# A fused low-rank linear layer on one core: part of the first load goes to GpSimd's DMA queue, and the matmul loop takes in its last round

## The chip, the cores and the metric

The kernel runs on one core of a Trainium2 chip. The core has a matrix engine (TensorE, PE in the profile), a vector engine (VectorE, DVE), a scalar engine (ScalarE, ACT), GpSimd (POOL) and SyncE (SP), which only issues transfers here. Sixteen DMA engines carry all transfers between the device memory and the core's own memory (SBUF, 128 partitions), whichever engine issues them. The metric is the device time of one execution in microseconds (us); less is better. The profile shows one execution, and its span runs from the first to the last instruction that the profiler recorded.

## The reference: what is computed

```
x_flat = x.reshape(-1, in_dim)            # 32768 x 256, float32
y = x_flat @ W                            # W: 256 x 256
lora_out = x_flat @ lora_A                # lora_A: 256 x 16
lora_out = lora_out * lora_E              # lora_E: 16 numbers
lora_out = lora_out @ lora_B              # lora_B: 16 x 256
y = y + scale * lora_out                  # scale is 1.0; y is written as float32
```

x and the result are 33.55 MB each. Everything else is small: W is 256 KB, lora_A and lora_B 16 KB each, lora_E 64 bytes.

## The kernel before: how the work is laid out

The low-rank branch is folded into the weights once, before the main work. TensorE transposes lora_A (L125), VectorE scales the transposed rows by lora_E and by scale (`ate`, L129), TensorE multiplies that by lora_B (L134), and VectorE adds W to it (`weff`, L138). After that the kernel is one matrix product of x with `weff`, in bf16.

The 32768 rows of x are cut into nine chunks, listed in `PLAN` as rows per partition: 32 rows per partition are 4 MB, 16 are 2 MB. A partition's rows of a chunk lie next to each other in device memory, so one partition's share of a chunk is one piece of 32 KB or 16 KB. Six buffers of SBUF (`slots`) hold the chunks, and the result overwrites the chunk in place, so a buffer is free for the seventh, eighth and ninth chunk only when the store of its first user has landed.

SyncE's DMA queue carries W, all nine loads and all nine stores, in the order in which SyncE issues them. The first six loads (`LEAD`, L106) are issued before the engines' common starting barrier; lora_A, lora_B and lora_E are issued by ScalarE (L102 to L105). Behind the barrier SyncE issues the store of a chunk when ScalarE has written its last group (L209, L210). The entry `AFTER = {2: [6, 7, 8]}` puts the last three loads behind the third store: each of them waits until the store that frees its buffer has landed (L212, L213). The order on the queue is thus: six loads, three stores, three loads, six stores.

A chunk is worked on in groups of four rows per partition, 64 groups in all. VectorE rounds two groups at a time to bf16 (`rounded`, L148). TensorE transposes a group (`transposed`, L162), VectorE copies the transposed group out of the accumulator memory (`copied`, L154), TensorE multiplies it by `weff` (`multiplied`, L173), and ScalarE copies the product back over the chunk (L201). TensorE's program is a loop of 15 rounds of four groups (L189), and the sixteenth round is written out behind the loop (L193 to L196). The counters `can_t`, `can_m` and `can_y` let TensorE wait on constants inside the loop.

A transfer adds sixteen to its semaphore when it is done, one for each DMA engine, and the trace has the time of each of these sixteen steps.

Of the kernel before, what the change touches and what calls it, by code (L numbers as in the profile page):

```python
# [3 lines left out]

PLAN = [32] * 5 + [16, 16, 32, 32]
ROWS, SLOTS = 32, 6
LEAD = 6
AFTER = {2: [6, 7, 8]}

G, ROUND = 4, 4  # L10

B_PARTS = [(0, 16)]
P = 128
FP32 = mybir.dt.float32
BF16 = mybir.dt.bfloat16
# [15 lines left out]
def kernel(tc, x, W, lora_A, lora_B, lora_E, scale, out):  # L31
    nc = tc.nc
    x_flat = x.flatten_outer_dims()
# [4 lines left out]
    KC = K // P  # L38
    assert K == M and sum(PLAN) * P == N
    starts = [sum(PLAN[:i]) * P for i in range(len(PLAN))]  # L40

    groups = [(i, r) for i, b in enumerate(PLAN) for r in range(0, b, G)]
    NG = len(groups)
    assert NG % ROUND == 0

    def rows_of(flat, i):
        b, r0 = PLAN[i], starts[i]
        return flat[r0:r0 + b * P, :].rearrange("(p b) k -> p b k", b=b)

    def sbuf(name, shape, dt):  # L50
        return nc.alloc_sbuf_tensor(name, shape, dt).ap()

    def psum(name, shape, dt):
# [4 lines left out]
    e_sb = sbuf("e_sb", [R, 1], FP32)  # L58
# [9 lines left out]
    b_sb = xb[1][:R, G:G + 2, :].rearrange("p g k -> p (g k)").bitcast(FP32)  # L68
# [4 lines left out]
    ps_aeb = psum("ps_aeb", [P, KC, M], FP32)  # L73

    s_w, s_a, s_b, s_e = (Count(nc, f"s_{k}") for k in "wabe")
    s_ld = [Count(nc, f"s_ld{i}") for i in range(len(PLAN))]
    s_st = [Count(nc, f"s_st{i}") for i in range(len(PLAN))]
    s_id, s_set, s_v, s_t, s_m, s_y = (
        Count(nc, k) for k in ("s_id", "s_set", "s_v", "s_t", "s_m", "s_y"))


    can_t, can_m, can_y = (nc.alloc_semaphore(k) for k in ("can_t", "can_m", "can_y"))

    def slot(i):
        return slots[i % SLOTS][:, :PLAN[i], :]

    def load(i):
        s_ld[i].by(nc.sync.dma_start(out=slot(i), in_=rows_of(x_flat, i)), 16)
# [4 lines left out]
    def spent(engine, count):  # L93
        engine.wait_ge(count.sem, count.total).then_inc(count.sem, -count.total)

    def take(sem):
        nc.tensor.wait_ge(sem, 1).then_inc(sem, -1)  # L97


    with tc.tile_critical(no_gpsimd_drain=True):  # L100
        s_w.by(nc.sync.dma_start(out=w_sb, in_=W.rearrange("(c p) m -> p c m", p=P)), 16)
        s_a.by(nc.scalar.dma_start(out=a_sb, in_=lora_A.rearrange("(c p) r -> p c r", p=P)), 16)  # L102
        for lo, hi in B_PARTS:
            s_b.by(nc.scalar.dma_start(out=b_sb[lo:hi, :], in_=lora_B[lo:hi, :]), 16)
        s_e.by(nc.scalar.dma_start(out=e_sb, in_=lora_E[:, None]), 16)  # L105
        for i in range(LEAD):  # L106
            load(i)
    tc.close()
    tc.compile()  # L109
# [4 lines left out]
        out=ident, in_=ident, compare_op=mybir.AluOpType.not_equal, fill=1.0, base=0,  # L114
# [3 lines left out]


    nc.vector.wait_ge(s_b.sem, s_b.total)  # L120
    s_v.by(nc.vector.tensor_copy(out=b_bf, in_=b_sb))  # L121
    nc.tensor.wait_ge(s_a.sem, 16)
    nc.tensor.wait_ge(s_id.sem, 3)
    for c in range(KC):
# [5 lines left out]
        out=ate, in0=ps_at, scalar1=e_sb, scalar2=float(scale),  # L130
# [11 lines left out]
    def rounded(t):  # L142
        i, r = groups[2 * t]
        if r == 0:
            nc.vector.wait_ge(s_ld[i].sem, 16)
        if t >= 2:
            nc.vector.wait_ge(s_t.sem, 2 * t - 2)
        nc.vector.tensor_copy(out=xb[t % 2], in_=slot(i)[:, r:r + 2 * G, :]).then_inc(can_t, 1)  # L148

    def copied(g):  # L150
        nc.vector.wait_ge(s_t.sem, g + 1)
        if g >= 2:
            nc.vector.wait_ge(s_m.sem, g - 1)
        nc.vector.tensor_copy(out=xt[g % 2], in_=ps_xt[g % 2]).then_inc(can_m, 1)  # L154


    def transposed(k):
        if k % 2 == 0:
            take(can_t)
        for j in range(G):  # L160
            for c in range(KC):
                done = nc.tensor.transpose(  # L162
                    ps_xt[k % 2][:, j, c, :],
                    xb[k // 2 % 2][:, k % 2 * G + j, c * P:(c + 1) * P],
                    ident_bf)
        done.then_inc(s_t.sem, 1)

    def multiplied(k):
        take(can_m)
        take(can_y)  # L170
        for j in range(G):
            for c in range(KC):
                done = nc.tensor.matmul(  # L173
                    ps_y[k % 2][:, j, :], xt[k % 2][:, j, c, :], weff[:, c, :],
                    start=(c == 0), stop=(c == KC - 1))
        done.then_inc(s_m.sem, 1)

    rounded(0)
    nc.vector.wait_ge(s_v.sem, 3)
    rounded(1)  # L180
    nc.scalar.sem_inc(can_y, 2)
    for t in range(NG // 2):
        copied(2 * t)
        copied(2 * t + 1)
        if t + 2 < NG // 2:
            rounded(t + 2)

    transposed(0)
    with nc.tensor.Fori(0, NG // ROUND - 1):  # L189
        for k in range(ROUND):  # L190
            transposed((k + 1) % ROUND)
            multiplied(k)
    for k in range(ROUND):  # L193
        if k + 1 < ROUND:
            transposed(k + 1)
        multiplied(k)  # L196
    s_t.total = s_m.total = NG

    for g, (i, r) in enumerate(groups):
        nc.scalar.wait_ge(s_m.sem, g + 1)  # L200
# [21 lines left out]
    nc.tensor.wait_ge(can_y, 1).then_inc(can_y, -1)  # L222
    for count in [s_y] + s_st:
        spent(nc.sync, count)


# [33 lines left out]
```

## Time and profile before

| what | before |
|---|---|
| median of 3 runs (lowest, highest) | 164.19 us (164.1, 164.44) |
| the profiled execution, its own time | 164.33 us |
| its span | 162.9 us |
| busy share of TensorE / VectorE / ScalarE / GpSimd | 57% / 49% / 41% / 1% |
| moved by DMA, mean rate over the span | 67.45 MB, 414 GB/s |
| first 4 MB load, issue to landing (issued at 1.4 us) | 12.6 us |
| ScalarE's last copy ends | 130.9 us |
| last store, issue to landing (issued at 130.9 us) | 32.0 us |

The profiled execution took 1.43 us more than its span. The page draws the span as forty equal slices of 4.07 us; a digit is the busy share of an engine in that slice in tenths. The row "DMA" is the mean over the sixteen DMA engines, and "GB/s" is what they moved. The table of stretches gives the same for any stretch of the span; there a packet of a transfer is counted whole in the stretch in which it starts. A packet is here the piece of one partition: 32 KB or 16 KB for x.

### The profile page before, as it was taken

The page shows a single profiled execution, that of the slowest core. Times are in us where ns is not written, and L with a number is a line of the kernel's source. Part 1 is how long each engine was busy: PE and PEld are TensorE (multiplying, and loading weights), DVE is VectorE, ACT ScalarE, POOL GpSimd, SP SyncE. Part 2 cuts the span into 40 slices and gives each one's busy share as a digit, 9 for nine tenths or more (in the row PEclk, how much of TensorE's full clock was granted, in tenths as well). Part 3 has the DMA queues.
Part 4 walks back from the last instruction along what each step waited for, and adds up shares of the span by engine and source line. Part 5 has one row for each costly group of instructions (what it writes and reads, how often), then busy time and mean ns, then how long its engine had stood idle before and what let it go on. Part 6 is the DMA issues. An engine that isn't in the chain of part 4 may idle for free. (4 is left out here: it accounts for less than half of the span.)

```text
span 162.9 us, 2599 instructions
## 1 busy us (share of the span) xinstructions
PE 92.5 (57%) x1028; PEld 81.5 (50%) x1028; DVE 79.5 (49%) x99; ACT 66.1 (41%) x65; POOL 1.0 (1%) x7
## 2 busy tenths in 40 slices
PE   0112999999999999997000049599999800000000
PEld 0002789888988898896000038498889600000000
DVE  0025878898889888882000083588987300000000
ACT  0300277777777777777000004467777710000000
POOL 0100000000000000000000000000000000000000
PEclk9999999999999999999855556999999965555555
DMA  6999899999998999999999999999999999999991
GB/s 197 390 491 410 386 507 394 394 499 394 426 469 382 326 451 418 467 402 442 442 394 426 467 402 467 420 426 459 410 442 426 410 404 438 451 442 426 442 451 64
DMA packets 3205, 67.45 MB, mean 414 GB/s; under 512 B 625, under 2 KB 897, under 8 KB 897
## 3 DMA queue, kind: packets, MB, share of 16 engines
q1 hardware_dynamic: 2864, 67.37, 97.1%
q10 hardware_dynamic: 336, 0.03, 0.2%
q8 instruction: 1, 0.02, 0.0%
q14 instruction: 4, 0.02, 0.0%
HBM read 33.85 MB, written 33.55 MB: 414 GB/s over the span
## 5 line engine op out<-in xcount | busy, mean ns | idle before, releaser
L201 ACT COPY xy<-psum_y 128x1024 f32<-128x1024 f32 x64 | 64.8, 1012 | 59.3 <-PE psum_y L173 59.3
L173 PE MATMUL psum_y<-weff,xt 128*128 128x256 bf16 x512 | 68.7, 279 | 23.1 <-PEq L97 21.6
L173 PEld LDWEIGHTS psum_y<-weff,xt 128*128 128x128 bf16 x512 | 47.5, 99 | 31.2 <-issue 25.7
L154 DVE COPY xt<-psum_xt 128x1024 bf16<-128x1024 bf16 x64 | 43.8, 687 | 15.3 <-PE psum_xt L162 15.1
L148 DVE CAST xb<-xy 128x2048 bf16<-128x2048 f32 x32 | 38.9, 1218 | 24.0 <-DMA xy<-in_x_dram 24.0
L162 PE MATMUL psum_xt<-ident_bf,xb 128*128 128x128 bf16 x512 | 40.5, 224 | 5.1 <-PEq L97 5.1
L162 PEld LDWEIGHTS psum_xt<-ident_bf,xb 128*128 128x128 bf16 x512 | 35.4, 101 | 7.2 <-issue 5.5
L125 PE MATMUL ps_at<-ident,a_sb 128*16 128x128 f32 x2 | 0.6, 394 | 6.7 <-POOL ident_bf L117 6.7
L121 DVE CAST b_bf<-xb 16x256 bf16<-16x256 f32 x1 | 0.3, 282 | 6.7 <-DMA xb<-in_lora_B_dram 6.7
L201 ACT ACT_TABLE_LOAD x1 | 1.3, 1283 | 5.5 <-PEq L109 5.5
L125 PEld LDWEIGHTS ps_at<-ident,a_sb 128*16 128x16 f32 x2 | 0.1, 88 | 6.7 <-issue 6.7
L134 PE MATMUL ps_aeb<-b_bf,ate 16*128 16x256 bf16 x2 | 0.6, 404 | 2.4 <-DVE ate L129 2.4
L134 PEld LDWEIGHTS ps_aeb<-b_bf,ate 16*128 16x128 bf16 x2 | 0.1, 106 | 2.9 <-DVE ate L129 2.9
L129 DVE TENSOR_SCALAR ate<-ps_at,e_sb 16x256 bf16<-16x256 f32 x1 | 0.5, 471 | 2.2 <-DMA e_sb<-in_lora_E_dram 2.2
L138 DVE TENSOR_TENSOR weff<-xb,ps_aeb 128x512 bf16<-128x512 f32 x1 | 0.7, 687 | 0.8 <-PE ps_aeb L134 0.8
L113 POOL TENSOR_SCALAR_AFFINE_SELECT ident<-ident 128x128 f32<-128x128 f32 x1 | 0.3, 292 | 0.2 <-POOL ident L111 0.2
L117 POOL CAST ident_bf<-ident 128x128 bf16<-128x128 f32 x1 | 0.3, 291 | 0.1
L111 POOL MEMSET ident<- 128x128 f32 x1 | 0.2, 204 | 5.0 <-POOLq L109 5.0
L241 POOL MEMSET const-bfloat16-1.0<- 128x1 bf16 x1 | 0.1, 101 | 0.0
L241 POOL MEMSET const-uint8-127<- 128x1 uint8 x1 | 0.1, 101 | 0.0
L241 POOL MEMSET const-float32-0.0<- 128x1 f32 x1 | 0.1, 98 | 0.2 <-issue 0.2
L241 POOL MEMSET const-float32-1.0<- 128x1 f32 x1 | 0.1, 98 | 0.0
## 6 DMA issues: line engine op xcount, KB each, us to landing
xy<-in_x_dram SPq DMA_DIRECT2D x7, 4096.0 KB, 24.6
out_dram<-xy SPq DMA_DIRECT2D x7, 4096.0 KB, 36.6
xy<-in_x_dram SPq DMA_DIRECT2D x2, 2048.0 KB, 40.1
out_dram<-xy SPq DMA_DIRECT2D x2, 2048.0 KB, 35.9
xb<-in_W_dram SPq DMA_DIRECT2D x1, 256.0 KB, 3.0
a_sb<-in_lora_A_dram ACTq DMA_DIRECT2D x1, 16.0 KB, 3.2
xb<-in_lora_B_dram ACTq DMA_DIRECT2D x1, 16.0 KB, 5.3
e_sb<-in_lora_E_dram ACTq DMA_DIRECT2D x1, 0.1 KB, 7.2
```

Of the source, the lines that this page charges most:

```text
L113: s_id.by(nc.gpsimd.affine_select(out=ident, in_=ident, compare_op=mybir.AluOpType.not_equal, fill=1.0, base=0, pattern=[[-1, P]], channel ...
L117: s_id.by(nc.gpsimd.tensor_copy(out=ident_bf, in_=ident))
L125: at_done = nc.tensor.transpose(ps_at[:, c, :], a_sb[:, c, :], ident)
L129: s_v.by(nc.vector.tensor_scalar(out=ate, in0=ps_at, scalar1=e_sb, scalar2=float(scale), op0=mybir.AluOpType.mult, op1=mybir.AluOpType.mult))
L134: aeb_done = nc.tensor.matmul(ps_aeb[:, c, :], ate[:, c, :], b_bf, start=True, stop=True)
L138: s_v.by(nc.vector.tensor_add(out=weff, in0=w_sb, in1=ps_aeb))
L148: nc.vector.tensor_copy(out=xb[t % 2], in_=slot(i)[:, r:r + 2 * G, :]).then_inc(can_t, 1)
L154: nc.vector.tensor_copy(out=xt[g % 2], in_=ps_xt[g % 2]).then_inc(can_m, 1)
L162: done = nc.tensor.transpose(ps_xt[k % 2][:, j, c, :], xb[k // 2 % 2][:, k % 2 * G + j, c * P:(c + 1) * P], ident_bf)
L173: done = nc.tensor.matmul(ps_y[k % 2][:, j, :], xt[k % 2][:, j, c, :], weff[:, c, :], start=(c == 0), stop=(c == KC - 1))
L201: y = nc.scalar.copy(out=slot(i)[:, r:r + G, :], in_=ps_y[g % 2])
L241: nc = _bacc.Bacc("TRN2", target_bir_lowering=False, num_devices=1)
```

## The change

`PLAN` puts a chunk of 16 rows first, and has one such chunk in place of two side by side further on: the six loads of the lead are 16, 32, 32, 32, 32, 32 rows instead of 32, 32, 32, 32, 32, 16, the last three 16, 32, 32 as before. lora_E is loaded in two parts: its first four numbers by GpSimd's queue, the other twelve by ScalarE's as before. The first chunk is loaded in three parts. GpSimd's queue loads the last eight of its sixteen rows for partitions 0 to 119; SyncE's queue loads the first eight rows of all partitions, and then the last eight rows of partitions 120 to 127. VectorE waits for both of GpSimd's transfers ahead of its first operation, the cast of lora_B, and for both of SyncE's ahead of its first rounding. TensorE's loop runs 16 rounds, and nothing is written out behind it; its last round transposes one group too many, from data that is not used, for which VectorE adds one to `can_t` at its end. At the end GpSimd sets back the semaphore of its transfers.

```diff
-PLAN = [32] * 5 + [16, 16, 32, 32]
+PLAN = [16] + [32] * 5 + [16, 32, 32]
...
-B_PARTS = [(0, 16)]
+SW_ROWS, SW_PARTS, E_SW = 8, 120, 4
...
+    s_sw, s_seen = Count(nc, "s_sw"), Count(nc, "s_seen")
...
-        for lo, hi in B_PARTS:
-            s_b.by(nc.scalar.dma_start(out=b_sb[lo:hi, :], in_=lora_B[lo:hi, :]), 16)
-        s_e.by(nc.scalar.dma_start(out=e_sb, in_=lora_E[:, None]), 16)
-        for i in range(LEAD):
+        s_b.by(nc.scalar.dma_start(out=b_sb, in_=lora_B), 16)
+        s_e.by(nc.scalar.dma_start(out=e_sb[E_SW:, :], in_=lora_E[E_SW:, None]), 16)
+        x0, to0, b0 = rows_of(x_flat, 0), slot(0), PLAN[0] - SW_ROWS
+        s_sw.by(nc.gpsimd.dma_start(out=e_sb[:E_SW, :], in_=lora_E[:E_SW, None]), 16)
+        s_sw.by(nc.gpsimd.dma_start(out=to0[:SW_PARTS, b0:, :], in_=x0[:SW_PARTS, b0:, :]), 16)
+        s_ld[0].by(nc.sync.dma_start(out=to0[:, :b0, :], in_=x0[:, :b0, :]), 16)
+        s_ld[0].by(nc.sync.dma_start(out=to0[SW_PARTS:, b0:, :], in_=x0[SW_PARTS:, b0:, :]), 16)
+        for i in range(1, LEAD):
             load(i)
...
     nc.vector.wait_ge(s_b.sem, s_b.total)
+    s_seen.by(nc.vector.wait_ge(s_sw.sem, s_sw.total))
...
-            nc.vector.wait_ge(s_ld[i].sem, 16)
+            nc.vector.wait_ge(s_ld[i].sem, 16 if i else s_ld[i].total)
...
+    nc.vector.sem_inc(can_t, 1)
...
-    with nc.tensor.Fori(0, NG // ROUND - 1):
+    with nc.tensor.Fori(0, NG // ROUND):
         for k in range(ROUND):
             transposed((k + 1) % ROUND)
             multiplied(k)
-    for k in range(ROUND):
-        if k + 1 < ROUND:
-            transposed(k + 1)
-        multiplied(k)
-    s_t.total = s_m.total = NG
+    s_t.total, s_m.total = NG + 1, NG
...
+    spent(nc.gpsimd, s_seen)
+    nc.gpsimd.inc_swdge_sem([s_sw.sem], [s_sw.total], mode="sub")
```

## The prediction, made before the result was known

> **What bounds the kernel now.** I read the page from its busy shares to its DMA rows, then the chain that ended last, then the table of stretches for the end of the span.
>
> ```profile
> PE 92.5 (57%) x1028; PEld 81.5 (50%) x1028; DVE 79.5 (49%) x99; ACT 66.1 (41%) x65; POOL 1.0 (1%) x7
> ...
> DMA  6999899999998999999999999999999999999991
> GB/s 197 390 491 410 386 507 394 394 499 394 426 469 382 326 451 418 467 402 442 442 394 426 467 402 467 420 426 459 410 442 426 410 404 438 451 442 426 442 451 64
> ...
> q1 hardware_dynamic: 2864, 67.37, 97.1%
> ```
>
> No engine is above 57%, while the DMA engines are busy from the second slice to the last but one, and SyncE's queue alone (q1) fills 97.1% of all sixteen. The timeline shows that nothing computes at the end:
>
> ```profile
> 129.85 1.01 ACT L201 COPY xy<-psum_y 128x1024 f32<-128x1024 f32 x1 [0.17 <-PE psum_y L173]
> 130.89 0.33 SPq L91 DMA_DIRECT2D out_dram<-xy  x1
> ```
>
> The last result is ready at 130.9 us and its store lands 32.0 us later, at 162.9, because it stands behind other stores. So the time is: when the transfers start, plus what the slowest of the sixteen DMA engines has to move. The last slice (64 GB/s) says that they do not end together. The table of stretches, in steps of 0.4 us, shows the last starts (the last two columns are DMA share and GB/s):
>
> ```profile
> 158.80:159.20 0.40, 0.00 (x0) 0.00 (x0) 0.00 (x0) 0.00 (x0) 0.00 (x0) 0.50 0.57 246
> 159.20:159.60 0.40, 0.00 (x0) 0.00 (x0) 0.00 (x0) 0.00 (x0) 0.00 (x0) 0.50 0.38 164
> 159.60:160.00 0.40, 0.00 (x0) 0.00 (x0) 0.00 (x0) 0.00 (x0) 0.00 (x0) 0.50 0.39 164
> 160.00:160.40 0.40, 0.00 (x0) 0.00 (x0) 0.00 (x0) 0.00 (x0) 0.00 (x0) 0.50 0.00 0
> 160.40:160.80 0.40, 0.00 (x0) 0.00 (x0) 0.00 (x0) 0.00 (x0) 0.00 (x0) 0.50 0.19 82
> 160.80:161.20 0.40, 0.00 (x0) 0.00 (x0) 0.00 (x0) 0.00 (x0) 0.00 (x0) 0.50 0.00 0
> 161.20:161.60 0.40, 0.00 (x0) 0.00 (x0) 0.00 (x0) 0.00 (x0) 0.00 (x0) 0.50 0.19 82
> ```
>
> A packet of 32 KB takes 1.213 us (median of the trace's 1792) and is counted where it starts, so one packet is 1.213/(16 x 0.4) = 0.19. The reader sees one engine start its last packet after 161.2 and one after 160.4, where most had finished. The last store's semaphore tells it exactly: of its sixteen steps the first comes at 159.79, the ninth at 160.33, the last four at 160.84, 161.49, 162.06 and 162.89. Call the last three engines C, B and A. A is 0.83 behind B and some 2.6 behind the middle.
>
> Why they are late stands in the records of single packets. On A packets took about 1.30 us instead of 1.213 in two stretches (58.9 to 77 and 114 to 131, some fourteen each, so 2 x 14 x 0.09 = 2.5 us); I have no cause for it. B and C carry fetches of program code (8 KB or 16 KB) at 47.3, 130.6 and 133.1 us; the one at 47.3 cost 0.31 us, and the packet behind it took 1.81 instead of 1.21.
>
> One stretch also shows a common loss, in the sixth load, whose pieces are 16 KB:
>
> ```profile
> 3.00:52.00 49.00, 36.90 (x409) 32.23 (x410) 34.22 (x43) 25.57 (x25) 0.79 (x3) 1.00 1.01 431
> ...
> 54.50:57.50 3.00, 2.88 (x35) 2.56 (x33) 2.78 (x4) 2.38 (x3) 0.00 (x0) 1.00 1.06 311
> 57.50:87.00 29.50, 18.71 (x222) 16.84 (x220) 14.73 (x19) 14.23 (x15) 0.00 (x0) 0.89 1.00 433
> ```
>
> Its first step comes 5.57 us after the one of the load before (52.48 to 58.05), where 2 MB otherwise take 4.85: 0.7 us for all engines. The other 16 KB load (87 to 92) dipped for 1.5 us to about 412 GB/s, which is 0.07 us.
>
> **The change part by part.**
>
> *The first chunk through GpSimd's queue.* A transfer of 128 partitions gives each engine eight packets (1792 packets of 32 KB = 14 transfers x 16 x 8). If shares of eight partitions stay, 120 partitions fill fifteen engines, and one gets none. That engine is spared 8 packets of 8 KB. An 8 KB packet takes 0.309 us (the code fetches at 47.3, 105.3 and 133.1; 0.531 at most, ahead of the span), so 8 x 0.309 = 2.47 us. The eight rows of partitions 120 to 127 go back to SyncE's queue as eight packets, on eight engines if one each: +0.31 on half of them. If the spared engine is A, it lands at 162.89 - 2.47 + (0 or 0.31) = 160.4 to 160.7, and B ends the kernel: 0.83 us earlier, less 0 or 0.31; I take +0.15, as it is eight of sixteen.
> The price of a packet of GpSimd's queue is not in the trace. Its ends are 0.309 (nothing lost; with no gain below it, since the bytes are the same) and 0.531, which is 8 x 0.222 = 1.8 us on fifteen engines. I take 0.309, the price beside the same traffic.
> Smaller pieces: each engine now has 16 packets of 0.309 for the first chunk where it had 8 of 0.611: +0.06 us.
>
> [...]
>
> *Start.* The first W packet starts at 2.0 us, all engines carry data by 2.8, and SyncE's issues at 1.4 to 4.4 run ahead of the data. GpSimd is free at 0.44, but waits for the same go-ahead as SP and ACT (0.9). Its data can come earlier than 2.0 only if its issue is faster than theirs: I take 0, with -0.5 as the far end. One SyncE issue more (0.3 to 0.5 us) lies beside the data of load 0 (2 x 2.5 us on the engines).
>
> *VectorE's new wait.* Behind it on VectorE stand the cast of lora_B, `ate`, `weff` and all roundings; TensorE and ScalarE wait for these. If each of GpSimd's eight packets stands behind a 32 KB packet of SyncE's, it takes 8 x (0.309 + 1.213) = 12 us: done by some 17 us, first rounding some 5 later, at 22 (14.03 before). What must be in time is the third store, when the DMA engines reach it: loads end at 58, stores of 2 and 4 MB take 14.6, so at 72.6. Before, it came 38.0 us after the first rounding, for 24 groups; for 20 groups that is 31.7, so 54. It costs nothing unless the wait lasts 18 us more. GpSimd's identity matrix (5.46 before) and the common barrier can slip by microseconds under the same cover.
>
> *The order of chunks.* Lead 22 MB as before. The first store is 2 MB instead of 4, so the seventh load is issued 4.85 us earlier (69.3 before) and lands as much earlier; the ninth is issued with two loads (14.6 us) ahead of it, as before, and six stores are issued behind it at once. The last store is ready near 126, and the engines reach it at 150: no gap. The sixth load now has pieces of 32 KB, like the ninth, whose passage to the stores lost nothing; a 16 KB pattern now stands at the start. The common loss of 0.7 may go (-0.7), or come again in load 0 (0); I take -0.3, near the middle, as both readings have one row.
>
> *TensorE's loop.* 64 matmuls with their weight loads leave the program; one unused transposition (8 x 76 ns = 0.6 us) comes after 126, where nothing waits for it. Fewer code bytes may save a fetch on B: between 0 and -0.9 (0.31 and the stretched packet); I take 0, since no row says whose fetch it is.
>
> *GpSimd's end.* Its reset waits for VectorE's early mark and is over more than 100 us before the end.
>
> Sum: -0.83 + 0.15 + 0.06 - 0.3 = -0.9 us. The profiled execution took 164.33 (162.9 and 1.43 around it), 0.14 above the median, so I take the sum off the median: 164.19 - 0.9 = 163.3.
>
> **The rivals.**
>
> *The wrong engine is spared.* Then A ends the kernel as before, plus 0 or 0.31, plus 0.06, less the 0.3: 164.19 - 0.1 = 164.1 (163.4 to 164.6). For it: no row names A's number. Against: 2.47 us fit A's delay of 2.6. It is also what happens if the slow engine changes with the execution, but three runs within 0.34 us speak for a steady one.
> [...]
>
> *GpSimd's packets are dear (the other side).* Place: the first 10 us on fifteen engines, B among them. At 0.531 a packet: 164.19 - 0.9 + 1.8 = 165.1. It decides from 0.309 + 0.9/8 = 0.42 us a packet. For it: 8 KB fetches at the start of the program took 0.34 to 0.53. Against: those in mid-run took 0.309.
>
> *The change does not do what it says:* the 120 partitions are spread over all sixteen engines or over few. Over sixteen it ends like the first rival; over eight, each would carry 2.47 us more: 166.
>
> **How the numbers follow.** A spared: 0.55, at 163.3 (own range 162.5 to 163.8). Wrong engine: 0.23. Dear packets: 0.17. Few engines: 0.05. 0.2% (0.33 us) is about what can be told from no change. Faster: 0.54 of the first, 0.07 of the second, together 0.61. Within: 0.01 and 0.10, 0.11. Slower: 0.06 of the second, 0.17 and 0.05, 0.28. The range runs from 162.4 (A spared, a fetch on B saved as well) to 164.9, which leaves out the dearest packets and few engines.
>
> **What would show it.** Right: the last store's steps end within 2.3 us instead of 3.1, the last lone packet of the table of stretches is gone, and a new queue shows about 0.98 MB in packets near 0.31 us; the first rounding may be later than 14 us without any price. The sixth load's slice (326 GB/s) rises to 430. The forecast is wrong if one engine still stands 2.6 behind the middle, if packets of the new queue take over 0.42, or if the first GB/s slices drop.

## The result, and the profile after

The changed kernel takes 170.12 us (median of four runs, 169.58 to 170.47), the kernel before 164.25 beside it. The ratio is 1.0354, with a 95% interval of 1.032 to 1.0387: 5.9 us slower, where 0.9 us less was forecast, and above the range's end of 164.9. The profiled execution took 169.58 us, its span is 168.2, 5.3 more than before.

The page after, with the rows that answer to those of before (engines, DMA share and rate by slices of 4.2 us, the two queues that carry x, and the idle time of GpSimd):

```profile
PE 93.0 (55%) x1036; PEld 82.5 (49%) x1036; DVE 79.5 (47%) x99; ACT 66.1 (39%) x65; POOL 2.2 (1%) x9
...
DMA  5999998989999999999999999999999999999980
GB/s 155 344 316 306 308 395 374 491 382 475 397 452 421 436 407 436 452 405 468 397 417 436 479 390 477 390 468 397 460 413 452 413 454 393 444 456 405 467 366 39
...
q1 hardware_dynamic: 2880, 66.39, 94.6%
q0 software_dynamic: 176, 0.98, 2.0%
...
L118 POOL MEMSET ident<- 128x128 f32 x1 | 0.2, 205 | 22.3 <-POOLq L116 22.3
```

The engines work as long as before, and the DMA engines are as busy as before. But in slices 2 to 5 (4 to 21 us) they move 306 to 344 GB/s at that same busy share: each packet takes longer. The table of stretches after shows where it ends (last two columns: DMA share and GB/s):

```profile
10.00:14.00 4.00, 0.00 (x0) 0.00 (x0) 0.00 (x0) 0.00 (x0) 0.00 (x0) 1.00 0.95 289
14.00:22.00 8.00, 0.00 (x0) 0.00 (x0) 0.00 (x0) 0.00 (x0) 0.00 (x0) 1.00 1.00 304
24.00:50.00 26.00, 20.67 (x208) 17.42 (x208) 18.78 (x24) 12.42 (x12) 0.78 (x3) 1.00 0.98 423
```

The same stretches before:

```profile
10.00:14.00 4.00, 0.31 (x2) 0.00 (x0) 0.69 (x1) 0.00 (x0) 0.00 (x0) 1.00 0.93 401
14.00:22.00 8.00, 6.42 (x62) 5.55 (x63) 6.56 (x8) 2.15 (x3) 0.00 (x0) 1.00 1.05 455
```

The records of packets say which packets were slow. GpSimd's start to move at 6.0 us and the last starts at 21.9. Between 7 and 22 us they took 0.434 us in the middle, but SyncE's 32 KB packets, which alternate with them, took 1.72 instead of 1.213. Of the sixteen steps of GpSimd's transfer of x one comes at 14.67, from the engine that had no packet, and the other fifteen at 22.7 to 24.2. That engine's own 32 KB packets were slow as well, though nothing alternated with them: its step of the second load comes at 21.55, the next at 23.96, and none of the 32 KB packets that start between 7 and 22 us, on any engine, took less than 1.51 us.

The end of the span, in the same view as before:

```profile
162.40:162.80 0.40, 0.00 (x0) 0.00 (x0) 0.00 (x0) 0.00 (x0) 0.00 (x0) 0.50 0.38 164
162.80:163.20 0.40, 0.00 (x0) 0.00 (x0) 0.00 (x0) 0.00 (x0) 0.00 (x0) 0.50 2.08 901
...
165.20:165.60 0.40, 0.00 (x0) 0.00 (x0) 0.00 (x0) 0.00 (x0) 0.00 (x0) 0.50 0.19 82
165.60:166.00 0.40, 0.00 (x0) 0.00 (x0) 0.00 (x0) 0.00 (x0) 0.00 (x0) 0.50 0.00 0
166.00:166.40 0.40, 0.00 (x0) 0.00 (x0) 0.00 (x0) 0.00 (x0) 0.00 (x0) 0.50 0.00 0
166.40:166.80 0.40, 0.00 (x0) 0.00 (x0) 0.00 (x0) 0.00 (x0) 0.00 (x0) 0.50 0.19 82
```

Two engines still start a packet late and alone (0.19 is one packet). The last store's steps come at 162.41 (one engine), 164.31 (the next), 164.53 to 164.55 in the middle, and 166.21, 166.55 and 168.19 last. So one engine was spared, and it is some 2 us ahead; the late one was not it, and stands 3.7 behind the middle instead of 2.6.

The start of the computation is late; that had no price, as the section on the prediction works out:

```profile
24.98 0.20 POOL L118 MEMSET ident<- 128x128 f32 x1 [22.32 <-POOLq L116]
...
28.75 2.36 DVE L156 CAST xb<-xy 128x2048 bf16<-128x2048 f32 x2
```

The common barrier opens when GpSimd's transfer has landed (its last step comes at 24.17 us, the first instruction behind the barrier at 24.98), and the first rounding comes at 28.75 us (14.03 before). From 24 us on the DMA rate is back, and the transfers have no gap up to the last store.

### The profile page after: what moved, and what is told of

Same layout as the page of the kernel before. It is cut to its first block, busy times and chain, and to the rows that moved or that the text cites. A ratio compares the mean times of both kernels' runs of the same rounds, so it can differ in the third digit from the quotient of the medians.

```text
span 168.2 us, 2627 instructions
## 1 busy us (share of the span) xinstructions
PE 93.0 (55%) x1036; PEld 82.5 (49%) x1036; DVE 79.5 (47%) x99; ACT 66.1 (39%) x65; POOL 2.2 (1%) x9
## 5 line engine op out<-in xcount | busy, mean ns | idle before, releaser
L170 PE MATMUL psum_xt<-ident_bf,xb 128*128 128x128 bf16 x520 | 41.6, 226 | 2.1 <-PEq L100 2.1
L170 PEld LDWEIGHTS psum_xt<-ident_bf,xb 128*128 128x128 bf16 x520 | 36.2, 102 | 4.2 <-issue 2.5
L109 POOL DMA_DIRECT2D e_sb<-in_lora_E_dram x1 | 0.6, 642 | 1.0 <-PEq L116 1.0
L110 POOL DMA_DIRECT2D xy<-in_x_dram x1 | 0.5, 538 | 0.0
```

What stands on the lines that cost most here:

```text
L109: s_sw.by(nc.gpsimd.dma_start(out=e_sb[:E_SW, :], in_=lora_E[:E_SW, None]), 16)
L110: s_sw.by(nc.gpsimd.dma_start(out=to0[:SW_PARTS, b0:, :], in_=x0[:SW_PARTS, b0:, :]), 16)
L170: done = nc.tensor.transpose(ps_xt[k % 2][:, j, c, :], xb[k // 2 % 2][:, k % 2 * G + j, c * P:(c + 1) * P], ident_bf)
```

## The experiments

Three theories were put up first. Theory 1: GpSimd's queue itself slows the transfers. Theory 2: any second queue whose packets alternate with SyncE's does. Theory 3: the first chunk's 16-row layout is slow to read. All experiments are edits of the changed kernel, and every time stands beside runs of the kernel before on the same chip (164.2 to 164.4 us). The diffs show only the lines that matter, and `...` marks what is left out. They are against the changed kernel, but for e10_nine_each (against e1_sync_queue) and e8_staircase (against e4_no_gpsimd). Where GpSimd's queue is not used, ScalarE loads lora_E whole, and VectorE's wait for GpSimd's transfers is gone.

**Without GpSimd's queue.**

```diff
-        s_sw.by(nc.gpsimd.dma_start(out=e_sb[:E_SW, :], ...
-        s_sw.by(nc.gpsimd.dma_start(out=to0[:SW_PARTS, b0:, :], ...
-        s_ld[0].by(nc.sync.dma_start(out=to0[:, :b0, :], ...
-        s_ld[0].by(nc.sync.dma_start(out=to0[SW_PARTS:, b0:, :], ...
-        for i in range(1, LEAD):
+        for i in range(LEAD):
```

> The changed kernel without GpSimd's queue: the first chunk of 16 rows is loaded whole by SyncE, lora_E whole by ScalarE; the new order of chunks and the loop stay. Theory 1 (GpSimd's queue itself slows the transfers of all engines) and theory 2 (any second queue whose packets alternate with SyncE's does) both say that the loss of the first 24 us is gone: first chunk and second chunk land near 9 and 19 us, and the time is 163.5 us, 0.7 below before, because the sixth load's common loss is gone. Theory 3 (the 16-row layout of the first chunk is slow to read beside the next) says 168 or more.

Measured: 164.41 us, ratio 1.0011 (0.9998 to 1.0025). The slow start is gone (8.73 to 9.38 us for the first chunk, 18.4 to 19.1 for the second), which takes theory 3 away. The new order of the chunks and the closed loop together are worth nothing. The common loss in the sixth load did not go: it stands at 55 to 58 us (rates down to 305 GB/s), though its pieces are now 32 KB. My 163.5 missed by that.

**The same pieces on SyncE's queue.**

```diff
-        s_sw.by(nc.gpsimd.dma_start(out=to0[:SW_PARTS, b0:, :], in_=x0[:SW_PARTS, b0:, :]), 16)
         s_ld[0].by(nc.sync.dma_start(out=to0[:, :b0, :], in_=x0[:, :b0, :]), 16)
+        s_ld[0].by(nc.sync.dma_start(out=to0[:SW_PARTS, b0:, :], in_=x0[:SW_PARTS, b0:, :]), 16)
```

> All parts of the first chunk as in the changed kernel, but the 120 partitions go through SyncE's queue, behind its first part; lora_E whole by ScalarE. One engine is still spared eight packets. Theories 1 and 2: no slow stretch, 163.2 to 164 us; the lower end if the spared engine is the late one, A. Theory 3: 168 or more.

Measured: 167.3 us, ratio 1.0177 (1.0139 to 1.0215). Neither theory 1 nor theory 2 allows this: there is one queue only for x, and still the transfer is slow. From 7 to 10 us the rate is 229 GB/s, and the 8 KB packets take 0.59 us (middle, 7 to 9.5 us), twice the 0.309 of the first part of the same chunk:

```profile
3.00:6.00 3.00, 0.00 (x0) 0.00 (x0) 0.00 (x0) 0.00 (x0) 0.00 (x0) 1.00 1.06 368
6.00:7.00 1.00, 0.00 (x0) 0.00 (x0) 0.30 (x1) 0.42 (x1) 0.27 (x2) 1.00 1.19 352
7.00:10.00 3.00, 1.18 (x4) 0.25 (x4) 0.81 (x2) 0.86 (x1) 0.51 (x2) 1.00 1.02 229
```

The spared engine ends 2.1 us ahead here (160.43 against 162.56), and again the late one is another (166.15).

**The 120 partitions on ScalarE's queue.**

```diff
-        s_sw.by(nc.gpsimd.dma_start(out=to0[:SW_PARTS, b0:, :], in_=x0[:SW_PARTS, b0:, :]), 16)
+        s_ld[0].by(nc.scalar.dma_start(out=to0[:SW_PARTS, b0:, :], in_=x0[:SW_PARTS, b0:, :]), 16)
```

> The 120 partitions go through ScalarE's queue instead of GpSimd's, at the same time as SyncE's loads. Theory 1: 163.2 to 164.4 us, SyncE's 32 KB packets at 1.21 us beside the 8 KB ones. Theory 2: 168 to 171 us, 32 KB packets at 1.6 to 1.9 us until the eight 8 KB packets of each engine are through.

Measured: 170.46 us, ratio 1.0385 (1.0355 to 1.0415), as slow as the changed kernel, with the same picture: 8 KB packets at 0.467, 32 KB packets at 1.75 us. So it is not GpSimd's queue; theory 1 falls. Theory 2 is right on the number, but cannot explain the run before it.

**GpSimd's transfer with nothing beside it.**

```diff
+        nc.sync.wait_ge(s_sw.sem, s_sw.total)
         for i in range(1, LEAD):
             load(i)
```

> The changed kernel, but SyncE waits for GpSimd's transfers before it issues the second load, so that GpSimd's eight packets on each engine run with nothing beside them. Theory 1: they stay slow, 0.4 us or more a packet, and the end is 168 us or more. Theory 2: 0.309 us a packet; the DMA engines idle 2 to 4 us for the wait and the new issue, and the time is 166 to 167.5 us, below the changed kernel's 170.

Measured: 170.31 us, ratio 1.037 (1.0346 to 1.0393). With nothing alternating, GpSimd's packets are still slow: 0.58 us in the middle, 210 GB/s from 7 to 10 us, of fifteen engines that move 397 at 0.309 us a packet (15 x 8192 B / 0.309 us). SyncE's last 8 KB packet ends at 7.47 us, and the 49 packets of GpSimd that start from 8.9 to 11 us still took 0.575 in the middle and 0.52 at least. So the small transfer of partitions 120 to 127 is not the cause either. That is theory 1's number, after theory 1 had fallen. What e1, e2 and e3 have in common is neither a queue nor the alternation, but the shape: 120 partitions.

**Two new theories.** An engine's share of 128 partitions and its share of 120 need not be the same partitions. I assume shares of eight neighbours for the 120; the trace names neither partitions nor any place inside SBUF. Theory 4 is that two engines then write through one entrance of SBUF at a time and each gets half, as the packets of e1_sync_queue and e3_alone got about half (0.59 and 0.58 us instead of 0.309). Half of 397 to 432 GB/s (15 x 8192 B / 0.309 us, 16 x 32768 B / 1.213 us) is 199 to 216. That there is such an entrance, and which engines would meet at it, is my conjecture; no run shows it. Theory 5 is that the source is slow to read: with shares of eight partitions, neighbouring engines read 128 KB apart (8 x 16 rows of 1 KB), which would have to be farther than in a load of 128 partitions.

**The source rows close together.**

```diff
-        s_ld[0].by(nc.sync.dma_start(out=to0[:SW_PARTS, b0:, :], in_=x0[:SW_PARTS, b0:, :]), 16)
+        dense = x_flat[:SW_PARTS * SW_ROWS, :].rearrange("(p b) k -> p b k", b=SW_ROWS)
+        s_ld[0].by(nc.sync.dma_start(out=to0[:SW_PARTS, b0:, :], in_=dense), 16)
```

> As e1_sync_queue, but the 120-partition transfer reads 960 rows that lie next to each other (rows 0 to 959 of x) instead of eight rows out of every sixteen; the destination and the shares of the engines stay. The last eight rows of the first chunk are then other rows than the reference's. Theory 4: as slow as e1_sync_queue, 166.7 to 167.8 us. Theory 5: 164 to 164.8 us.

Measured: 167.39 us, ratio 1.0183 (1.0157 to 1.0209), as e1_sync_queue; 8 KB packets at 0.615 us. These other source addresses change nothing, which speaks against theory 5.

**Two halves of 64 partitions.**

```diff
-        s_ld[0].by(nc.sync.dma_start(out=to0[:SW_PARTS, b0:, :], in_=x0[:SW_PARTS, b0:, :]), 16)
-        s_ld[0].by(nc.sync.dma_start(out=to0[SW_PARTS:, b0:, :], in_=x0[SW_PARTS:, b0:, :]), 16)
+        for lo in (0, 64):
+            s_ld[0].by(nc.sync.dma_start(out=to0[lo:lo + 64, b0:, :], in_=x0[lo:lo + 64, b0:, :]), 16)
```

> As e1_sync_queue (all on SyncE's queue), but the last eight rows go as two transfers of 64 partitions, 0 to 63 and 64 to 127: the source rows are those of the 128-partition load, all engines get the same number of bytes, and only which engine writes which partition at which time differs. Theory 4 (the shares of neighbouring partitions make two DMA engines write through one entrance of SBUF at a time, and each gets half): the 1 MB moves at about 200 to 216 GB/s, 8 KB packets at 0.6 us, and the kernel ends 2.4 us above e4_no_gpsimd, at 166.5 to 167.3 us. Theory 5 (the wide source stride of shares of eight partitions is slow to read): with shares of four it is as fast as ever, 164 to 164.6 us. [...]

Measured: 166.63 us, ratio 1.0129 (1.0105 to 1.0153), 2.2 us above e4_no_gpsimd; the 8 KB packets take 0.61 us, twice 0.309. All engines carry the same bytes here and none is spared. Theory 4 was right with its number, and theory 5 was not; what the engines meet at, the run does not show. From 7 to 10 us:

```profile
6.00:7.00 1.00, 0.00 (x0) 0.00 (x0) 0.00 (x0) 0.00 (x0) 0.00 (x0) 1.00 1.22 336
7.00:10.00 3.00, 1.04 (x4) 0.25 (x4) 0.78 (x2) 1.28 (x1) 0.79 (x3) 1.00 1.04 229
```

The DMA share is full (1.04) and the rate is about half: 229 GB/s, where e4_no_gpsimd moves 508 and e6_all_partitions 437 in the same stretch. A busy share of DMA engines is here no measure of what they move.

**GpSimd's queue with all 128 partitions.** This is the changed kernel with one thing undone, the split at partition 120.

```diff
-SW_ROWS, SW_PARTS, E_SW = 8, 120, 4
+SW_ROWS, SW_PARTS, E_SW = 8, 128, 4
...
-        s_ld[0].by(nc.sync.dma_start(out=to0[SW_PARTS:, b0:, :], in_=x0[SW_PARTS:, b0:, :]), 16)
```

> The changed kernel, but GpSimd's queue carries the last eight rows of all 128 partitions, so each of sixteen engines keeps the partitions that it has in every other load, and none is spared. Theory 4 (two engines that write through one entrance of SBUF halve each other): nothing meets although the two queues alternate; GpSimd's 8 KB packets at 0.31 us, SyncE's 32 KB packets at 1.21, and the time is 163.6 to 164.7 us. Theory 6 (GpSimd's queue beside SyncE's has a price of its own): 166 us or more.

Measured: 164.55 us, ratio 1.0019 (1.0007 to 1.0032). The loss is gone, with GpSimd's queue, its four numbers of lora_E, the wait on VectorE, the late barrier and the alternation all in place. From 7 to 22 us all of GpSimd's packets of the middle 80% took 0.309 us, and SyncE's 1.213. The two queues and the stretches, to compare with 289 and 304 after, and with 229 in e1_sync_queue and e7_halves from 7 to 10 us:

```profile
q1 hardware_dynamic: 2864, 66.32, 95.2%
q0 software_dynamic: 176, 1.05, 1.5%
```

```profile
7.00:10.00 3.00, 0.00 (x0) 0.00 (x0) 0.00 (x0) 0.00 (x0) 0.00 (x0) 1.00 1.02 437
10.00:14.00 4.00, 0.00 (x0) 0.00 (x0) 0.00 (x0) 0.00 (x0) 0.00 (x0) 1.00 1.12 483
14.00:22.00 8.00, 0.59 (x2) 0.12 (x2) 0.32 (x2) 1.28 (x1) 0.78 (x3) 1.00 1.02 438
```

0.98 MB in 2.0% of sixteen engines' time became 1.05 MB in 1.5%. The queue has no price here; the shape had it.

**Partitions nine apart, three tries.** If only engines that meet lose, shares that never meet should be fast. That shares nine partitions apart never meet is my assumption; no run shows it.

```diff
-        s_ld[0].by(nc.sync.dma_start(out=to0[:SW_PARTS, b0:, :], in_=x0[:SW_PARTS, b0:, :]), 16)
-        s_ld[0].by(nc.sync.dma_start(out=to0[SW_PARTS:, b0:, :], in_=x0[SW_PARTS:, b0:, :]), 16)
+        for lo in range(9):
+            s_ld[0].by(nc.sync.dma_start(out=to0[lo::9, b0:, :], in_=x0[lo::9, b0:, :]), 16)
```

> As e1_sync_queue, but the last eight rows go as nine transfers on SyncE's queue, each of every ninth partition (14 or 15 partitions, one packet an engine), so that neighbouring engines write partitions nine apart. The source stride between engines is even wider than in e1_sync_queue (144 KB instead of 128). Theory 4: no two engines meet, 8 KB packets at 0.31 us and the rate above 370 GB/s, and the time is 164 to 165 us (thirteen or fourteen engines carry one packet more). Theory 5: slow as e1_sync_queue, 166.7 us or more.

Measured: 167.33 us, ratio 1.0174 (1.015 to 1.0199). The time tells nothing on the theories: SyncE needed 7.5 us for the nine issues, and the DMA engines ran dry (DMA share 0.60 from 7 to 10 us). The 8 KB packets took 0.342 us in the middle there, near 0.309, but with engines idle fewer could meet. The issues:

```profile
1.96 7.49 SPq L111 DMA_DIRECT2D xy<-in_x_dram  x9
9.49 2.67 SPq L91 DMA_DIRECT2D xy<-in_x_dram  x5
```

```diff
-SW_ROWS, SW_PARTS, E_SW = 8, 120, 4
+SW_ROWS, SW_PARTS, E_SW = 8, 126, 4
```

> As e1_sync_queue, but split at partition 126 instead of 120. [...]

Measured: 166.17 us, ratio 1.0149 (1.0096 to 1.0202): less than e1_sync_queue, but 1.8 above e4_no_gpsimd. The packets from 6 to 7 us took 0.346 in the middle (0.381 in e1_sync_queue, 0.446 in e7_halves), and later 0.61, like theirs:

```profile
6.00:7.00 1.00, 0.00 (x0) 0.00 (x0) 0.30 (x1) 0.64 (x1) 0.48 (x2) 1.00 1.03 377
7.00:10.00 3.00, 1.19 (x4) 0.25 (x4) 1.02 (x2) 0.65 (x1) 0.30 (x2) 1.00 1.06 243
```

If shares of nine partitions keep the engines apart, as I assumed, theory 4 did not allow this. A reason that would fit it is that engines which are not at the same packet of their share meet after all, and then stay together; that is argued, not shown. A plainer reading is not excluded: that a transfer whose shares are not those of 128 partitions is slow, whoever meets whom. Two engines were spared (first steps of the last store at 159.33 and 159.51, the third at 161.41), so fourteen engines carried the 126 packets; neither of the two was the late one (164.55).

The same edit in the changed kernel, on GpSimd's queue:

> As the changed kernel, on GpSimd's queue, but split at partition 126. [...]

Measured: 168.36 us, ratio 1.0268 (1.0233 to 1.0302). But on this queue the 126 partitions did not go to fourteen engines. GpSimd's 126 packets start in eight rounds (18, 16, 16, 16, 16, 16, 15 and 13 packets), some 2.1 us apart, where fourteen engines would need nine rounds, and all sixteen steps of the transfer come between 22.04 and 23.44 us. So sixteen engines carried it; none was spared, and an engine's share was about eight packets again. No step of the last store stands apart in front either (162.95, 163.25, 163.27). SyncE's 32 KB packets took 1.67 us until 22, GpSimd's 0.381, much as in the changed kernel. The run therefore does not tell GpSimd's packets meeting each other from their meeting SyncE's.

**A staircase to number the late engine.**

```diff
+        lo = 0
+        for k in (14, 12, 10, 8, 6, 4, 2):
+            s_x.by(nc.scalar.dma_start(out=slots[0][lo:lo + k, 16:, :], in_=rows_of(x_flat, 0)[lo:lo + k, :, :]), 16)
+            lo += k
```

> e4_no_gpsimd with seven extra loads on ScalarE's queue at the start, 16 KB a partition into memory that nobody uses, of 14, 12, 10, 8, 6, 4 and 2 partitions. [...]

The seven loads were to give the engines different numbers of extra packets, and so to tell by the delays of the last store which one is late.

Measured: 177.14 us in a single run, and no answer. The extra loads of neighbouring partitions, 0.9 MB, slowed everything until 35 us (163 to 168 GB/s at 8 to 10 us), and the steps of the last store spread over 7.2 us in no order that names an engine. The late engine's number stays open.

## Why the prediction was wrong, step by step

**What failed** is the price of a packet of GpSimd's queue, and what I counted as its place. I bounded it by 0.309 to 0.531 us and took 0.309, "the price beside the same traffic", which came from single fetches of program code. The traffic beside it was the same, but a transfer of 120 partitions is not made of such fetches. GpSimd's own packets took 0.434, within the bounds, but the cost lay mostly on SyncE's, which the sum left at 1.213: 1.72 instead of 1.213 for some eight packets on each of sixteen engines, 4 us, with GpSimd's own 1 us (8 x 0.125) on top. Against e4_no_gpsimd the second load comes 5.5 us later (24.2 and 18.7, middle of its steps). e6_all_partitions shows that this is the split at partition 120 alone: 164.55 with 128, 170.12 with 120 and 8. Why a split by partitions is slow is not shown: theory 4, a conjecture, gives the right price in e7_halves (0.61 us a packet), but not every detail (see what stays open).

**The rival of dear packets** had the right side, and its threshold (0.42 us) was passed, but its mechanism was wrong: it made the queue dear, and the queue is not (0.309 in e6_all_partitions). By it the time was 165.1 at most, and 164.3 at the measured 0.434 (164.19 - 0.9 + 8 x 0.125). It left out that another queue's packets can become slow as well, as SyncE's did here (1.72 us instead of 1.213). I gave the whole slow side 0.28 and put the end of the range below it. No row of before showed a transfer of another shape than 128 partitions at size; the bound should have said that. The signs of being wrong that the prediction names all came: packets over 0.42, first slices at 306 to 344 GB/s, and an engine far behind the middle at the end.

**The spared engine.** That one engine gets none if shares of eight partitions stay was right: one engine ends 1.9 us ahead. That it is A was wrong, in the changed kernel, in e1_sync_queue and in e10_nine_each. The end before shows by how much an engine is late, but not which one it is. So even without the loss, the gain of 0.83 would have been missed, as the first rival (164.1) said.

**Spreading the transfers over two queues** gained nothing: e6_all_partitions, where the spreading is left beside the order of the chunks and the loop, is 1.0019 of before, +0.3 us, and the order and the loop without the spreading (e4_no_gpsimd) are 1.0011.

**The smaller terms.** The common loss of 0.7 us in the sixth load did go in the changed kernel (9.72 us from the fifth load's first step to the sixth's, 51.09 to 60.81), but not for the size of the pieces, since e4_no_gpsimd with the same 32 KB kept it (47.58 to 57.71). So where this term came out, it was by luck. The loop gained nothing, as predicted, and the new order of the chunks gained nothing where I had taken 0.3 (e4_no_gpsimd). VectorE's wait was longer than worked out (first rounding at 28.75, not 22), because GpSimd's transfer landed at 24.2 instead of 17; from there to the first rounding it is 4.6 us, near the 5 that I took. It had no price, as predicted: the third store was issued at 62.2 us, and the second store still occupied the engines until its steps at 75.3 to 78.9. e6_all_partitions too has a late barrier, at 20 us, without loss.

**The sum after.** In the span: +5.5 at the second load, -0.7 for the common loss, -0.6 that the middle engines regained up to the end and that no row places (164.5 against 160.3, +4.2 in all), and +1.1 because the last engine stands 3.7 behind them instead of 2.6: 5.3, the difference of the spans.

**What stays open** is why the split is slow, which engine is late, and why. Three things do not fit theory 4 as it stands. e10_nine_each was slow (0.61 us a packet) with shares that I took never to meet. Of fifteen engines that meet in pairs one has no partner, but in e3_alone only the last of the 97 packets of GpSimd that start from 7 us on took less than 0.52 us (0.426), so no engine ran its share at 0.309. And in the changed kernel the spared engine's 32 KB packets were slow throughout (none of those from 7 to 22 us took less than 1.51), though it carried no 8 KB packet of GpSimd's; by theory 4 another engine must have met it all that time, and no row shows one.

## What to carry to other kernels

In these runs a DMA over 64, 120 or 126 partitions moved about half the bytes in the same busy time (229, 229 and 243 GB/s from 7 to 10 us in e7_halves, e1_sync_queue and e10_nine_each, 437 over 128 in e6_all_partitions), and those on a second queue slowed SyncE's loads beside them (1.67 to 1.75 us a 32 KB packet instead of 1.213): compare the rate with the busy share, and the packets' durations with those of a full transfer, before a transfer is cut by partitions. Cut by rows instead, which cost 0.2% here (e6_all_partitions, against 0.1% without any cut in e4_no_gpsimd). Before an engine that is late is relieved, find out which one it is.

## What the runs showed that was not expected

The loss of 0.4 to 1.0 us near the end of the first six loads went with engines that ran in step. The first fifteen steps of the fifth load lay within 0.39 to 0.47 us in the kernel before, e3, e4, e6 and e9, and all of these had it (rates down to 230 to 305 GB/s); they lay 0.69 us apart in e7, 0.9 in e11 and 2 us or more in the changed kernel, e1, e2, e5, e8 and e10, and none of these did. Why is not shown.

GpSimd's transfer held the common barrier: with it, the first instruction behind the barrier comes at 24.98 us (20.03 in e6_all_partitions) instead of 5.46.
